# Attention in a two-layer trunk: the product of probabilities and V taken by key block for all 512 queries of a head

## The chip, the cores and the metric

The kernel runs on one core of a Trainium2 chip. The metric is the device time of one execution in microseconds. TensorE (PE) multiplies matrices into PSUM, VectorE (DVE), ScalarE (ACT) and GpSimd (POOL) do the work between the products, and SyncE (SP) issues the transfers.

## The reference

A trunk of two layers on 2048 frames of width 1024. Layer A is a gMLP mixer, which the change doesn't touch. Layer B is band attention with 16 heads of 64 channels: each chunk of 64 queries sees its own chunk and the eight before it, with a bias by clipped distance.

```python
def one_chunk(args):
    c, qc = args
    start = c * CHUNK
    kc = lax.dynamic_slice_in_dim(k_pad, start, B_BAND, axis=1)
    vc = lax.dynamic_slice_in_dim(v_pad, start, B_BAND, axis=1)
    sc = jnp.einsum('bqhd,bkhd->bhqk', qc, kc).astype(jnp.float32) + bias
    valid = (m + start) >= B_LEFT_PAD
    sc = jnp.where(valid[None, None, None, :], sc, NEG_INF)
    p = jax.nn.softmax(sc, axis=-1).astype(vc.dtype)
    return jnp.einsum('bhqk,bkhd->bqhd', p, vc)
...
return (o * jax.nn.silu(z)) @ w_out
```

All is float32, and the values need that accuracy.

## The kernel before

**Number format.** PE works on float32 values cut into a high and a low part (types F32R, made by a cast on ACT and a subtraction on DVE). A large product is three matmuls: high by high, low by high, high by low (`mm3`, lines 113 to 115, where most of PE's instructions therefore stand).

**Stages.** The mixer of layer A and the projection of V come first, up to some 1560 us. Then comes the attention, in four tiles of 512 queries (t), each with eight pairs of heads (p). For each pair there are eight steps u, four blocks of 128 queries for each of the two heads (`hd`, `qb`). A step issues, in this order of the source:

- `score`: the product of Q and K for the block two steps ahead (L1320), then on DVE the bias and the row maximum (L1328), on ACT the exponential with the row sum (L1335), on DVE its reciprocal (L1338), on POOL the scaling (L1339). A block of 128 queries sees 640 keys, in tile 0 fewer: 128 to 512, as there are no keys before.
- some products of the generators `ahead` (projections of Q, K and gate of the next pair, named pj) and `outs` (the output product of the tile before, named bo). They fill PE between the steps of the attention.
- `flip`: the probabilities of a block are transposed by PE in pieces of 128x128 into a scratch bank, of which there is one (`tp`, L1359); ACT casts them to the high part (L1362), DVE subtracts for the low part (L1363).
- at every second step `value`: the product with V (pv, lines 1380, 1381 and 1387).

**The product with V before.** It is taken for half a head, two blocks of queries (256 columns), with the half's own tile of transposed probabilities: [128, 2 parts, 6 key blocks, 256 queries]. There are two such tiles (tag PT, bufs=2). V stands as the stationary operand, 64 channels of the high part beside 64 of the low, so that the two halves of the result's partitions have to be added afterwards. The six key blocks of the half are not all seen by both query blocks: block 0 only by the first, block 5 only by the second. For tiles 1 to 3 these two are products of 2x128 columns which take the high and the low part side by side; the result is two sums (bank halves), the second of which holds only the low parts of the outer blocks:

```python
mm(po[:, :, 0:P], keys(0), pt[:, :, 0, 0:P], start=True, stop=False)
mm(po[:, :, P:256], keys(5), pt[:, :, 5, P:256], start=False, stop=False)
```

Then come four blocks of 256 columns for the high part and four for the low. ACT copies half of the partitions (L1399), DVE adds the other half (L1401) and then the two sums (L1406). In tile 0 all blocks are products of 256 columns; the part of block 5 that the first query block doesn't see is cleared by POOL (L1352), and L1401 alone makes the result.

**Order.** The program is written in the order above and a scheduler places the instructions of each engine by its own plan, so neighbours can change places. Every engine works off its queue in order; an instruction that waits holds up what is behind it. In tile 0 the weights of the projections come raw, are scaled on POOL (L184), cast on ACT (L199) and subtracted on DVE (L200), and the scaled ones are written back for the later tiles.

Of the kernel before, what the change touches and what calls it, by code (L numbers as in the profile page):

```python
# [17 lines left out]
P = 128  # L18
# [3 lines left out]
T = 512  # L22
# [11 lines left out]
def trunk_kernel(  # L34
# [19 lines left out]
    nc = tc.nc  # L54
# [42 lines left out]
    pmm = ctx.enter_context(tc.tile_pool(name="pmm", bufs=4, space=PSUM))  # L97
# [12 lines left out]
    mm, tpose = nc.tensor.matmul, nc.tensor.transpose  # L110
# [215 lines left out]
    with ExitStack() as actx:  # L326
# [492 lines left out]
        start = {}  # L819
# [8 lines left out]
        for n in range(6):  # L828
            for ph in PH:
# [4 lines left out]
                elif n > 2:  # L834
                    o = -13 if ph == 6 else -5
# [371 lines left out]
    with ExitStack() as bctx:  # L1207
        cb = bctx.enter_context(tc.tile_pool(name="cb", bufs=1, reuse_waits="tile"))
        sb = bctx.enter_context(tc.tile_pool(name="sb", bufs=2, reuse_waits="tile"))
# [6 lines left out]
        vtl = {}  # L1216
# [75 lines left out]
        pts = {}  # L1292
        og32s = {}
# [50 lines left out]
        def flip(t, p, u):  # L1344

            hd, qb = divmod(u, 4)
            h = 2 * p + hd
            g, qq = divmod(qb, 2)
            if qq == 0:
                pt = sb.tile([P, 2, 6, 256], F32R, tag="PT", name=f"pt{t}_{h}_{g}", bufs=2)  # L1350
                if t == 0:
                    nc.gpsimd.memset(pt[:, :, 5, 0:P].bitcast(F32), 0.0)  # L1352
                pts[t, h, g] = pt
            pt = pts[t, h, g]
            pr = prs[t, h, qb]
            b0 = 0 if t > 0 else 4 - qb
            tp = ptr.tile([P, KD, P], F32, tag="tr", name=f"tp{t}_{h}_{qb}")
            for b in range(b0, 5):
                tpose(tp[:, b, :], pr[:, b * P : (b + 1) * P], ident[:])  # L1359
            cs = slice(qq * P, (qq + 1) * P)  # L1360
            oh = pt[:, 0, b0 + qq : 5 + qq, cs]
            nc.scalar.copy(oh, tp[:, b0:5, :])  # L1362
            nc.vector.tensor_tensor(  # L1363
                pt[:, 1, b0 + qq : 5 + qq, cs], tp[:, b0:5, :], oh.bitcast(F32), op=ALU.subtract
            )

        def value(t, p, hd, g):

            h = 2 * p + hd
            pt = pts[t, h, g]  # L1370
            po = pmm.tile([P, 2, 256], F32, tag="mm", name=f"pv{t}_{h}_{g}")
            hs = slice(hd * P, hd * P + P)

            def keys(i):
                return vtl[t, p][:, 2 * g + i, hs]

            if t > 0:
                mm(po[:, :, 0:P], keys(0), pt[:, :, 0, 0:P], start=True, stop=False)  # L1380
                mm(po[:, :, P:256], keys(5), pt[:, :, 5, P:256], start=False, stop=False)
                blocks = range(1, 5)
            else:
                blocks = range(4 - 2 * g, 6)
            for j in range(2):
                for i in blocks:
                    mm(  # L1387
                        po[:, 0, :], keys(i), pt[:, j, i, :],
                        start=(t == 0 and j == 0 and i == blocks[0]),
                        stop=(j == 1 and i == blocks[-1]),  # L1390
                    )
            if hd == 0 and g == 0:
                og32s[t, p] = sb.tile([P, T], F32, tag="og32", name=f"og32_{t}_{p}", bufs=1)
            og32 = og32s[t, p]
            r, r2 = halves(hd)
            ot = sb.tile([P, 2, 256], F32, tag="ot", name=f"ot{t}_{h}_{g}", bufs=1)
            oq = og32[r, g * 256 : (g + 1) * 256]
            n = 2 if t > 0 else 1
            nc.scalar.copy(ot[r, :n, :], po[r2, :n, :])  # L1399
            o1 = ot[r, :, :] if t > 0 else oq  # L1400
            nc.vector.tensor_tensor(  # L1401
                o1, po[r, :n, :] if t > 0 else po[r, 0, :],
                ot[r, :n, :] if t > 0 else ot[r, 0, :], op=ALU.add,
            )
            if t > 0:
                nc.vector.tensor_tensor(oq, ot[r, 0, :], ot[r, 1, :], op=ALU.add)  # L1406
            if g == 0:
# [191 lines left out]
        def ahead(t, p):  # L1599

            if p + 1 < NPAIR:
                yield from project(t, p + 1)
                values(t, p + 1)
                if p == 0:
                    yield from gate(t, 0)
                yield from gate(t, p + 1)
                if t:
                    yield from some(outs[t - 1], SHARE[t][p])
            else:
                if t + 1 < NT:  # L1610
# [21 lines left out]
        before = None  # L1632
        for t in range(NT):
            for p in range(NPAIR):
                gen = ahead(t, p) if t + p else first
                total = steps_of(t, p) - (0 if t + p else 8)
                if t + 1 == NT and p + 1 == NPAIR:
                    last_open()
                per = 11 if p + 1 == NPAIR and t + 1 < NT else 16
                todo = []  # L1640
                if t == 0 and p in (2, 4):
                    todo = o_sums(p // 2 + 1, lambda n: half_tile("C", n, 4), lambda n: half_tile(
                        "S", n, 4, F32R
                    ))
# [24 lines left out]
                before = t, p  # L1669
        value(*before, 1, 1)  # L1670
        run(gen)
        while finals:
            finals.pop(0)()
# [58 lines left out]
```

## Time and profile before

| | |
|---|---|
| median of 3 runs | 2727.69 us (2720.04 to 2733.72) |
| profiled execution | 2731.61 us, span 2728.6 us |
| mean granted clock of TensorE | 0.986 |
| PE, DVE, ACT, POOL busy | 96%, 72%, 49%, 33% of the span |
| attention, tile 0 | from about 1560 to 1800 us |
| attention, tiles 1, 2, 3 | to about 2090, 2380, 2645 us |
| last output product | to the end |

The profile gives for each instruction its start and duration. Matmuls overlap in PE's pipeline, so that their durations add up to more than the time they take; the distance from one start to the next is what a matmul costs in a dense stretch. An idle time is shown with the instruction that ended it.

### The profile page before, as it was taken

How to read it: one execution, taken by the hardware profiler on the slowest of the kernel's cores; microseconds unless marked ns; L12 is line 12 of the kernel's file. 1: busy time of each engine (PE TensorE's matmuls, PEld its weight loads, DVE VectorE, ACT ScalarE, POOL GpSimd, SP SyncE). 2: the span in 40 equal slices, each digit the busy share in tenths (PEclk: the TensorE clock that was granted, in tenths of full speed). 3: DMA queues.
4: the chain of work that ended last, by engine and by line, in shares of the span. 5: the costliest groups of instructions: out<-in, count | busy, mean ns of one | idle time of the engine just before them, and what ended most of it. 6: DMA issues, size and time to landing. Idle time of an engine off the chain costs nothing. (4 is left out here: it accounts for less than half of the span.)

```text
span 2728.6 us, 38857 instructions
## 1 busy us (share of the span) xinstructions
PE 2630.1 (96%) x13216; PEld 2199.9 (81%) x13216; DVE 1961.0 (72%) x3097; ACT 1324.8 (49%) x2360; POOL 909.8 (33%) x906
## 2 busy tenths in 40 slices
PE   8999999999999999999989998999999999999997
PEld 7888888888888888888867776778887888788885
DVE  5655676676676669666677776677788778877787
ACT  5422242433424445332455465566656666666554
POOL 3512236142251414115143344322333223323243
PEclk9999999999999999999999999899999999999999
DMA  7899999989888879668667787766777667865567
GB/s 297 314 326 335 345 358 327 329 306 349 333 300 295 302 263 342 236 236 308 239 219 277 238 274 249 243 211 208 234 253 246 219 211 238 264 203 192 185 228 251
DMA packets 274773, 735.56 MB, mean 270 GB/s; under 512 B 29584, under 2 KB 61328, under 8 KB 274576
## 3 DMA queue, kind: packets, MB, share of 16 engines
q1 hardware_dynamic: 274576, 733.09, 77.9%
q8 instruction: 105, 1.72, 0.3%
q14 instruction: 92, 0.75, 0.1%
HBM read 540.56 MB, written 181.93 MB: 265 GB/s over the span
## 5 line engine op out<-in xcount | busy, mean ns | idle before, releaser
L113 PE MATMUL P<-T,S 128*128 128x512 f32 x1248 | 496.1, 398 | 2.7 <-ACT S L376 2.0
L115 PE MATMUL P<-T,S 128*128 128x512 f32 x1248 | 490.3, 393 | 0.0
L114 PE MATMUL P<-T,S 128*128 128x512 f32 x1248 | 489.1, 392 | 1.1 <-DVE T L379 1.1
L1339 POOL TENSOR_SCALAR pr<-pr,sl 128x640 f32<-128x640 f32 (+4 forms) x256 | 202.8, 792 | 553.9 <-DVE sl L1338 512.8
L113 PE MATMUL pj<-hh_b,wh_b 128*128 128x512 f32 x768 | 316.8, 412 | 7.7 <-ACT wh_b L199 6.7
L114 PE MATMUL pj<-hl_b,wh_b 128*128 128x512 f32 x768 | 307.4, 400 | 0.0
L115 PE MATMUL pj<-hh_b,wl_b 128*128 128x512 f32 x768 | 306.5, 399 | 0.0
L1335 ACT ACTIVATE pr<-pr,nm 128x640 f32<-128x640 f32 (+4 forms) x256 | 195.3, 763 | 222.4 <-DVE nm L1328 217.5
L115 PEld LDWEIGHTS P<-T,S 128*128 128x128 f32 x1248 | 235.4, 189 | 50.3
L113 PEld LDWEIGHTS P<-T,S 128*128 128x128 f32 x1248 | 235.9, 189 | 48.1 <-ACT S L376 2.3
L114 PEld LDWEIGHTS P<-T,S 128*128 128x128 f32 x1248 | 235.8, 189 | 46.9 <-DVE T L379 1.3
L1363 DVE TENSOR_TENSOR pt<-tp,pt 128x640 fp32r<-128x640 f32 (+4 forms) x256 | 188.8, 738 | 75.4 <-ACT pt L1362 73.1
L1328 DVE CUSTOM_DVE_ANT_0 pr<-s,bias 128x640 f32<-128x640 f32 (+4 forms) x256 | 188.2, 735 | 21.4 <-PE s L1320 15.6
L1362 ACT CAST pt<-tp 128x640 fp32r<-128x640 f32 (+4 forms) x256 | 158.6, 620 | 60.8 <-PE tp L1359 58.0
L1359 PEld LDWEIGHTS tp<-ident,pr 128*128 128x128 f32 x1120 | 135.1, 140 | 54.5 <-POOL pr L1339 15.9
L1359 PE MATMUL tp<-ident,pr 128*128 128x128 f32 x1120 | 165.8, 274 | 12.7 <-DVE pt L1363 6.5
L115 PEld LDWEIGHTS pj<-hh_b,wl_b 128*128 128x128 f32 x768 | 147.3, 192 | 32.6
L113 PEld LDWEIGHTS pj<-hh_b,wh_b 128*128 128x128 f32 x768 | 147.7, 192 | 27.5 <-ACT wh_b L199 8.3
L114 PEld LDWEIGHTS pj<-hl_b,wh_b 128*128 128x128 f32 x768 | 147.9, 193 | 17.3 <-issue 0.2
L1387 PE MATMUL pv<-pt,V 128*128 128x256 f32 x960 | 143.0, 289 | 11.2 <-ACT pt L1362 11.1
L200 DVE TENSOR_TENSOR wl_b<-raw_b,wh_b 128x1024 fp32r<-128x1024 f32 x96 | 122.9, 1280 | 42.4 <-ACT wh_b L199 41.2
L1387 PEld LDWEIGHTS pv<-pt,V 128*128 128x128 f32 x960 | 127.5, 193 | 14.9 <-ACT pt L1362 13.6
(291 smaller groups left out, 5941.5 us busy)
## 6 DMA issues: line engine op xcount, KB each, us to landing
S<-hsd SPq DMA_DIRECT2D x288, 512.0 KB, 5.5
rw<-in_w_a SPq DMA_DIRECT2D x108, 512.0 KB, 6.5
A<-ytd SPq DMA_DIRECT2D x72, 512.0 KB, 5.5
raw_b<-wk SPq DMA_DIRECT2D x72, 512.0 KB, 3.8
hsd<-S SPq DMA_DIRECT2D x56, 512.0 KB, 4.3
V<-vhd SPq DMA_DIRECT2D x56, 512.0 KB, 5.0
wh_bo<-ows SPq DMA_DIRECT2D x50, 512.0 KB, 4.5
wl_bo<-ows SPq DMA_DIRECT2D x50, 512.0 KB, 5.6
```

The costliest lines, as they stand in the source:

```text
L113: first = mm(ps, lh, rh, start=first, stop=False)
L114: mm(ps, lh, rl, start=False, stop=False)
L115: mm(ps, ll, rh, start=False, stop=last)
L200: tv(wl[:], raw[:], wh[:].bitcast(F32), op=sub)
L1328: nc.vector.tensor_tensor_reduce(out=pr[:, c0:].rearrange("p (a b) -> p a b", a=nseg), in0=ps[:, :nseg, :w], in1=bias[:, c0:].rearrange("p ...
L1335: nc.scalar.activation(pr[:, c0:], pr[:, c0:], AF.Exp, scale=-1.0, bias=nm[:], accum_out=sl[:])
L1339: nc.gpsimd.tensor_scalar(pr[:, c0:], pr[:, c0:], sl[:], 1.0, op0=ALU.mult, op1=ALU.mult)
L1359: tpose(tp[:, b, :], pr[:, b * P : (b + 1) * P], ident[:])
L1362: nc.scalar.copy(oh, tp[:, b0:5, :])
L1363: nc.vector.tensor_tensor(pt[:, 1, b0 + qq : 5 + qq, cs], tp[:, b0:5, :], oh.bitcast(F32), op=ALU.subtract)
L1387: mm(po[:, 0, :], keys(i), pt[:, j, i, :], start=(t == 0 and j == 0 and i == blocks[0]), stop=(j == 1 and i == blocks[-1]),)
```

## The change

One tile of transposed probabilities holds a whole head, [128, 5376]: the high parts of the four query blocks at 640 columns each, then the low parts (and room for a stride to run over). There is one such tile (bufs=1). `flip` writes each block to a contiguous stretch. `value` is called once for a head and goes by key block: block i of the eight (four in tile 0) is seen by query blocks q0 to q1, whose columns lie 512 apart in the tile, so that one product takes them all: 128, 256, 384 or 512 columns. High and low part of a block follow one another, and all is summed in one bank. The first block taken is one that all four query blocks see. Afterwards one copy on ACT and one addition on DVE, 64x512 each, make the head's result. The clearing on POOL falls away. The output rows (og32) get a second buffer.

In the loop, `value` of the first head stands ahead of `flip` at step 4, that of the second head ahead of `flip` at step 0 of the next pair; before, it stood behind `flip` at each even step.

```diff
-            g, qq = divmod(qb, 2)
-            if qq == 0:
-                pt = sb.tile([P, 2, 6, 256], F32R, tag="PT", name=f"pt{t}_{h}_{g}", bufs=2)
-                if t == 0:
-                    nc.gpsimd.memset(pt[:, :, 5, 0:P].bitcast(F32), 0.0)
-                pts[t, h, g] = pt
+            if qb == 0:
+                pts[t, h] = sb.tile([P, 5376], F32R, tag="PT", name=f"pt{t}_{h}", bufs=1)
...
-            oh = pt[:, 0, b0 + qq : 5 + qq, cs]
-            nc.scalar.copy(oh, tp[:, b0:5, :])
+            o = qb * 640
+            oh = pt[:, o + b0 * P : o + 640]
+            nc.scalar.copy(oh, tp[:, b0:5, :].rearrange("p a b -> p (a b)"))
...
-            if t > 0:
-                mm(po[:, :, 0:P], keys(0), pt[:, :, 0, 0:P], start=True, stop=False)
-                mm(po[:, :, P:256], keys(5), pt[:, :, 5, P:256], start=False, stop=False)
-                blocks = range(1, 5)
-            else:
-                blocks = range(4 - 2 * g, 6)
-            for j in range(2):
-                for i in blocks:
+            blocks = (3, 4, 0, 1, 2, 5, 6, 7) if t > 0 else (4, 5, 6, 7)
+            for i in blocks:
+                q0, q1 = max(0, i - 4), min(4, i + 1)
+                for j in range(2):
+                    o = j * 2560 + q0 * 512 + i * P
+                    rhs = pt[:, o : o + P]
+                    if q1 - q0 > 1:
+                        rhs = pt[:, o : o + (q1 - q0) * 512].rearrange("p (q c) -> p q c", c=512)
+                        rhs = rhs[:, :, 0:P]
                     mm(
-                        po[:, 0, :], keys(i), pt[:, j, i, :],
-                        start=(t == 0 and j == 0 and i == blocks[0]),
-                        stop=(j == 1 and i == blocks[-1]),
+                        po[:, q0 * P : q1 * P], vtl[t, p][:, i, hs], rhs,
+                        start=(i == blocks[0] and j == 0), stop=(i == 7 and j == 1),
                     )
...
-            nc.scalar.copy(ot[r, :n, :], po[r2, :n, :])
...
-            if t > 0:
-                nc.vector.tensor_tensor(oq, ot[r, 0, :], ot[r, 1, :], op=ALU.add)
+            nc.scalar.copy(ot[r, :], po[r2, :])
+            nc.vector.tensor_tensor(og32[r, :], po[r, :], ot[r, :], op=ALU.add)
...
+                    if u == 4:
+                        value(t, p, 0)
+                    elif u == 0 and before:
+                        value(*before, 1)
                     flip(t, p, u)
...
-                    if u % 2 == 0:
-                        if u:
-                            value(t, p, *divmod(u // 2 - 1, 2))
-                        elif before:
-                            value(*before, 1, 1)
```

More of the change, by code (lines that the diff above doesn't have):

```diff
@@ L1347, in flip @@
             h = 2 * p + hd
-            g, qq = divmod(qb, 2)
-            if qq == 0:
-                pt = sb.tile([P, 2, 6, 256], F32R, tag="PT", name=f"pt{t}_{h}_{g}", bufs=2)
-                if t == 0:
-                    nc.gpsimd.memset(pt[:, :, 5, 0:P].bitcast(F32), 0.0)
-                pts[t, h, g] = pt
-            pt = pts[t, h, g]
+            if qb == 0:
+                pts[t, h] = sb.tile([P, 5376], F32R, tag="PT", name=f"pt{t}_{h}", bufs=1)
+            pt = pts[t, h]
             pr = prs[t, h, qb]
@@ L1359, in flip @@
                 tpose(tp[:, b, :], pr[:, b * P : (b + 1) * P], ident[:])
-            cs = slice(qq * P, (qq + 1) * P)
-            oh = pt[:, 0, b0 + qq : 5 + qq, cs]
-            nc.scalar.copy(oh, tp[:, b0:5, :])
+            o = qb * 640
+            oh = pt[:, o + b0 * P : o + 640]
+            nc.scalar.copy(oh, tp[:, b0:5, :].rearrange("p a b -> p (a b)"))
             nc.vector.tensor_tensor(
-                pt[:, 1, b0 + qq : 5 + qq, cs], tp[:, b0:5, :], oh.bitcast(F32), op=ALU.subtract
+                pt[:, 2560 + o + b0 * P : 2560 + o + 640],
+                tp[:, b0:5, :].rearrange("p a b -> p (a b)"), oh.bitcast(F32), op=ALU.subtract,
@@ L1365, in flip, with value @@
             )
-        def value(t, p, hd, g):
+        def value(t, p, hd):
             h = 2 * p + hd
-            pt = pts[t, h, g]
-            po = pmm.tile([P, 2, 256], F32, tag="mm", name=f"pv{t}_{h}_{g}")
+            pt = pts[t, h]
+            po = pmm.tile([P, T], F32, tag="mm", name=f"pv{t}_{h}")
             hs = slice(hd * P, hd * P + P)
-            def keys(i):
-                return vtl[t, p][:, 2 * g + i, hs]
-            if t > 0:
-                mm(po[:, :, 0:P], keys(0), pt[:, :, 0, 0:P], start=True, stop=False)
-                mm(po[:, :, P:256], keys(5), pt[:, :, 5, P:256], start=False, stop=False)
-                blocks = range(1, 5)
-            else:
-                blocks = range(4 - 2 * g, 6)
-            for j in range(2):
-                for i in blocks:
-                    mm(
-                        po[:, 0, :], keys(i), pt[:, j, i, :],
-                        start=(t == 0 and j == 0 and i == blocks[0]),
-                        stop=(j == 1 and i == blocks[-1]),
-                    )
-            if hd == 0 and g == 0:
-                og32s[t, p] = sb.tile([P, T], F32, tag="og32", name=f"og32_{t}_{p}", bufs=1)
+            blocks = (3, 4, 0, 1, 2, 5, 6, 7) if t > 0 else (4, 5, 6, 7)
[7 more added lines that the diff above has]
+                        rhs = rhs[:, :, 0:P]
+                    mm(
+                        po[:, q0 * P : q1 * P], vtl[t, p][:, i, hs], rhs,
+                        start=(i == blocks[0] and j == 0), stop=(i == 7 and j == 1),
+                    )
+            if hd == 0:
+                og32s[t, p] = sb.tile([P, T], F32, tag="og32", name=f"og32_{t}_{p}", bufs=2)
@@ L1394, in value @@
             og32 = og32s[t, p]
             r, r2 = halves(hd)
[L1396 to L1404, printed above, removed]
@@ L1405, in value @@
-            if t > 0:
-                nc.vector.tensor_tensor(oq, ot[r, 0, :], ot[r, 1, :], op=ALU.add)
-            if g == 0:
+            ot = sb.tile([P, T], F32, tag="ot", name=f"ot{t}_{h}", bufs=1)
+            nc.scalar.copy(ot[r, :], po[r2, :])
+            nc.vector.tensor_tensor(og32[r, :], po[r, :], ot[r, :], op=ALU.add)
+            if hd == 0:
                 return
@@ L1669, in trunk_kernel @@
                 before = t, p
-        value(*before, 1, 1)
+        value(*before, 1)
         run(gen)
```

## The prediction

> **What bounds the kernel now.** I read the page's first two parts, then the table of stages, then the waits of TensorE in the first and in the later stages of the attention, and only then single products on the timeline. The page first: PE is busy nearly all of the span.
>
> ```profile
> PE 2630.1 (96%) x13216; PEld 2199.9 (81%) x13216; DVE 1961.0 (72%) x3097; ACT 1324.8 (49%) x2360; POOL 909.8 (33%) x906
> PEclk9999999999999999999999999899999999999999
> ```
>
> The change touches only the attention, which begins near 1560 us. The table of stages splits it: tile 0, tiles 1, 2, 3, and the tail. Columns after the stretch: its length, then busy time of PE, PEld, DVE, ACT, POOL, the granted clock and the DMA share.
>
> ```profile
> 1560.00:1800.00 240.00, 211.56 (x1054) 171.66 (x1052) 161.18 (x381) 138.33 (x311) 105.59 (x161) 0.94 0.77 248
> 1800.00:2090.00 290.00, 284.20 (x1615) 245.43 (x1615) 230.87 (x431) 178.94 (x320) 88.72 (x116) 0.99 0.72 233
> 2090.00:2380.00 290.00, 284.28 (x1624) 245.42 (x1623) 231.17 (x431) 180.90 (x323) 91.18 (x118) 0.99 0.72 232
> 2380.00:2645.00 265.00, 262.82 (x1516) 227.03 (x1515) 208.94 (x390) 161.31 (x294) 77.76 (x106) 1.00 0.62 198
> ```
>
> In tiles 1 to 3 PE is busy 98 to 99% at full clock and DVE, the next engine, some 80%: whatever PE has to do there is time. In tile 0 PE is idle 28 us and its clock is 0.94. The waits (microseconds in total, times, longest), first of 1560 to 1800, then of 1800 to the end:
>
> ```profile
> PE pv L1387 <- ACT pt L1362: 11.1, 5, 4.2
> PE tp L1359 <- DVE pt L1363: 3.5, 7, 0.9
> POOL pt L1352 <- PE pv L1387: 21.2, 13, 4.0
> ...
> PE s L1320 <- DVE nm L1328: 6.3, 5, 2.4
> PE tp L1359 <- DVE pt L1363: 3.0, 6, 0.9
> ```
>
> So tile 0 has waits at exactly the products that are changed; the later tiles have almost none on anything that is changed.
>
> **The products on PE.** A head of tiles 1 to 3 has 20 products of 256 columns (per half: two that take high and low part of an outer block side by side, then eight). After it has 16: four each of 512, 384, 256 and 128 columns. Both add up to 5120 columns. What counts is the step from one start to the next, because busy times of pipelined matmuls overlap. These rows of the timeline (start, duration) give the steps:
>
> ```profile
> 2003.17 1.12 PE L1387 MATMUL pv<-pt,V 128*128 128x256 f32 x8
> 2004.13 0.40 PE L113 MATMUL pj<-hh_b,wh_b 128*128 128x512 f32 x1
> ...
> 2005.52 0.45 PE L1320 MATMUL s<-K,Qh 128*128 128x320 f32 x2
> 2005.81 0.46 PE L1320 MATMUL s<-K,Ql 128*128 128x320 f32 x2
> 2006.10 0.39 PE L113 MATMUL pj<-hh_b,wh_b 128*128 128x512 f32 x1
> ...
> 1607.52 0.34 PE L1320 MATMUL s<-K,Qh 128*128 128x384 f32 x1
> 1607.70 0.35 PE L1320 MATMUL s<-K,Ql 128*128 128x384 f32 x1
> 1607.89 0.40 PE L113 MATMUL pj<-hh_b,wh_b 128*128 128x512 f32 x1
> ...
> 1747.53 0.39 PE L115 MATMUL pj<-hh_b,wl_b 128*128 128x512 f32 x1
> 1747.76 0.22 PE L1320 MATMUL s<-K,Qh 128*128 128x128 f32 x1
> 1747.82 0.28 PE L1320 MATMUL s<-K,Ql 128*128 128x128 f32 x1
> 1747.93 0.45 PE L113 MATMUL pj<-hh_b,wh_b 128*128 128x512 f32 x1
> 1748.21 0.39 PE L114 MATMUL pj<-hl_b,wh_b 128*128 128x512 f32 x1
> ```
>
> Columns of 256: (2004.13 - 2003.17) / 8 = 0.120 us. Of 512: the six products from 2004.13 to 2005.52 take 0.232 each. Of 320: (2006.10 - 2005.52) / 4 = 0.145. Of 384: 0.185 by the pair shown, 0.174 on the line between 320 and 512; I take 0.18. Of 128: a single step reads 0.06, but the next reads 0.11 and the product behind it starts late as well. From 1747.53 to 1748.21 there are two products of 512 and two of 128: 0.68 - 2 x 0.232 = 0.216, so 0.11 each. A product of 128 columns costs almost as much as one of 256, since the load of the next stationary tile does not fit under it; that is the cost that the change adds.
>
> The Trainium skill (TensorE: Matmul & The Clock Gate, Back-to-back issue gap) gives N / 2.4 + 2.5 ns between starts, 56 ns for 128 columns. By that estimate the sum below would be lower by some 12 us and the products a gain; the trace shows such a step only inside the pair and not for the pair as a whole, so the measurement decides.
>
> A head of tiles 1 to 3: before 20 x 0.120 = 2.40; after 4 x (0.232 + 0.18 + 0.12 + 0.11) = 2.57. That is +0.17 us for each of 48 heads, +8.1 us. A head of tile 0 has 12 products of 256 before (it multiplies a cleared block as well) and two of each width after: 1.44 against 1.28, -0.16 for each of 16 heads, -2.5 us. PE: **+5.6 us**. No row shows a 512-wide read in four pieces at a 2 KB pitch; two pieces of 128 (L1380) stand under the same 0.12 us, so I take no price. The 224 narrow products are the bound: at 0.06 each the sum falls by 11 to -6; at the price of 320 columns (0.145) it rises by 8 to +13.
>
> **What goes from DVE, ACT and POOL.** Groups of instructions (total, mean of one, idle before):
>
> ```profile
> L1401 DVE TENSOR_TENSOR ot<-pv,ot 64x512 f32<-64x512 f32 x96 | 65.7, 685 | 9.8 <-ACT ot L1399 8.2
> L1406 DVE TENSOR_TENSOR og<-ot 64x256 f32<-64x256 f32 x96 | 43.0, 448 | 2.7
> L1401 DVE TENSOR_TENSOR og<-pv,ot 64x256 f32<-64x256 f32 x32 | 13.4, 418 | 4.3 <-ACT ot L1399 3.8
> L1399 ACT COPY ot<-pv 64x512 f32<-64x512 f32 x96 | 55.9, 582 | 9.4 <-PE pv L1387 7.2
> L1399 ACT COPY ot<-pv 64x256 f32<-64x256 f32 x32 | 11.8, 368 | 3.7 <-PE pv L1387 2.9
> L1352 POOL MEMSET pt<- 128x256 f32 x32 | 10.1, 315 | 27.7 <-PE pv L1387 21.2 <-DVE Slv L286 3.2 <-issue 2.4
> ```
>
> DVE: 224 instructions, 122.1 us, become 64 additions of 64x512, 64 x 0.685 = 43.8: 78 us less. ACT: 67.7 us become 64 x 0.582 = 37.2: 30 us less. POOL loses 32 memsets of 10.1 us and the 21.2 us for which they stood at the head of its queue. Nearly all of it lies beside PE's work. What it can give is bounded by PE's waits on DVE in the later tiles, 6.3 + 3.0 us, most of which is not caused by the removed instructions; below nothing it cannot go, as no DVE instruction is added. I take **-2 us**. For POOL in tile 0: behind a waiting memset stand the normalisations (L1339) and the scaling of raw weights (L184), for which ACT and then PE wait. The 21.2 us are no price, since POOL was waiting for PE itself; I take **-2 us**, between nothing and the 11.1 us of PE's wait at the products.
>
> **The wait that moves.** The products stood behind the transposes of the next block; now they stand ahead of them, and with one probability tile (bufs=1) the copy of the next head's first block waits for the last product. That wait is free: on PE the products are already ahead of the transposes that the copy needs. Their second product needs the low half, so the subtraction on DVE, of the head's last block. In tiles 1 to 3 the transposes that stood at this place needed the same subtraction (the scratch bank of transposes is single), and they waited 3.0 us in all, so this costs nothing there. In tile 0 the four high products of 256 columns ran while DVE subtracted; now only one of 512 does, 0.48 - 0.23 = 0.25 us of cover less, on 16 heads at most 4 us; I take **+2 us**. Queued on ACT behind the copy that waits: exponentials and weight casts; they were behind the same transposes before.
>
> Also the spacing changes. Rows of PE and DVE in tile 1:
>
> ```profile
> 2016.50 0.71 PE L1359 MATMUL tp<-ident,pr 128*128 128x128 f32 x5
> 2016.96 0.48 PE L113 MATMUL bo<-wh_bo,Sho 128*128 128x512 f32 x1
> ...
> 2020.41 0.71 PE L1359 MATMUL tp<-ident,pr 128*128 128x128 f32 x5
> ...
> 2021.38 2.01 DVE L200 TENSOR_TENSOR wl_b<-raw_b,wh_b 128x1024 fp32r<-128x1024 f32 x1
> 2025.08 0.81 DVE L1363 TENSOR_TENSOR pt<-tp,pt 128x640 fp32r<-128x640 f32 x1
> 2026.04 0.74 PE L1359 MATMUL tp<-ident,pr 128*128 128x128 f32 x5 [0.38 <-DVE pt L1363]
> ```
>
> Between the transposes of neighbouring blocks lay some 3.4 us of other products (2016.96 to 2020.41), plus 1.2 us of products with V, ten at 0.120, at every second one. Now three come without and the fourth with 2.57. But the copy, the sum and the second addition (0.582, 0.685, 0.448) leave those windows too, so DVE's need falls with the cover. I price it at nothing; if DVE falls behind there, that is the second rival. SP's queue and the transfers keep their order in all that the sum uses; the second buffer of the output rows only removes a wait.
>
> **Sum.** +5.6 - 2 - 2 + 2 = +4 us. The profiled execution took 2731.61 us (span 2728.6 and 3.0 around it), so it would take 2735; it is 3.9 above the median 2727.69, to which the forecast belongs: **2732 us**. A measurement of this kernel can tell about 0.5%, 13.6 us, from no change, so the forecast is no change that can be told.
>
> **The rivals.**
> *Tile 0 recovers (faster).* With no memsets on POOL and fewer instructions on DVE, the 11.1 us at the products go, the transposes' 3.5 too, and half of what the clock lost (6% of 240 us, so 14, of which 7). That is -22, with the products' +5.6 it is -16 or so, in round numbers 2710. For it: 13 memsets waited for a product. Against: the longest waits of ACT in that tile are on raw weights (L184), which come by DMA and a POOL product of 1.9 us that remain.
>
> *DVE falls behind between value blocks (slower).* The rows above show the place: after the transposes at 2020.41, a weight split of 2.01 us comes ahead of the subtraction, which ends at 2025.89, and the next transposes wait although products with V lay between. Two blocks of each head lose 1.2 us of cover, 128 in all. It decides where the subtraction ends more than 3.4 us behind the transposes. If a quarter of them pay half of it, that is 32 x 0.6 = 19 us above the forecast: 2751. For it: such rows exist. Against: DVE has less to do, and only 13 such waits are in the whole stage now.
>
> *Fewer weight loads are a gain.* If each load of a stationary tile stood on the path, 256 products less at 0.11 us would give 28 us: 2700. The steps of 0.120 for 256 columns, load included, speak against it: a load is hidden there. The Trainium skill (TensorE: Matmul & The Clock Gate, The mechanism) says that loads overlap matmuls only in other row groups, which would put this rival first; the trace disagrees by those 0.120 us.
>
> **How the numbers follow.** Forecast 0.60 (of its own 2722 to 2742, from the narrow products' bounds, with 0.03 of it beyond the limit on the slow side); tile 0 recovers 0.12; weight loads 0.03; DVE behind 0.25. So faster 0.15, same 0.57, slower 0.28. The range leaves out about a tenth on either side: 2712 to 2752.
>
> **What would show it.** In the profile after: steps of 0.23, 0.18, 0.12 and 0.11 in the groups of products; PE's busy time in tiles 1 to 3 up by 2 to 3 us each with the same waits; DVE 78 and ACT 30 us less without a gain in the span. Wrong would be: steps of 0.06 behind the narrow products; a tile 0 that is more than 10 us shorter; or waits of transposes and products on the subtraction (L1363's successor) of over 15 us.

## The result and the profile after

| | before | after |
|---|---|---|
| median of 6 runs each | 2726.3 us (2720.0 to 2733.7) | 2711.9 us (2709.7 to 2715.6) |
| profiled execution, span | 2731.6, 2728.6 us | 2711.3, 2709.6 us |

The ratio is 0.9955, with a 95% interval of 0.9941 to 0.9968: 12 us faster by the ratio and 14 by the medians, where 2732 us was forecast. That is just below the forecast's range, and faster by more than the measurement is uncertain, though by a little less than 0.5%.

The first part of the page of the changed kernel has the DVE, ACT and POOL work gone as expected (DVE 79 us less, ACT 29, POOL 20):

```profile
PE 2624.9 (97%) x12960; PEld 2194.7 (81%) x12960; DVE 1882.2 (69%) x2937; ACT 1295.4 (48%) x2296; POOL 890.3 (33%) x874
```

The stages are cut here at the first transposes of each tile, since the tiles lie elsewhere after. Length, then busy time of PE, PEld, DVE, ACT, POOL, granted clock, DMA share, GB/s. First the kernel before, then after, tiles 0 to 3:

```profile
1569.00:1804.00 235.00, 209.01 (x1050) 170.21 (x1049) 161.28 (x381) 135.40 (x308) 102.78 (x158) 0.94 0.76 247
1804.00:2099.00 295.00, 289.22 (x1645) 249.42 (x1644) 235.24 (x441) 183.71 (x328) 90.65 (x119) 0.99 0.72 234
2099.00:2393.00 294.00, 287.85 (x1642) 248.12 (x1641) 234.87 (x439) 182.87 (x326) 91.21 (x119) 0.99 0.72 231
2393.00:2667.00 274.00, 267.87 (x1552) 231.43 (x1551) 217.55 (x408) 166.02 (x306) 89.68 (x117) 1.00 0.64 207
```

```profile
1566.00:1788.00 222.00, 205.19 (x995) 165.81 (x995) 159.81 (x365) 134.07 (x293) 94.12 (x127) 0.95 0.80 263
1788.00:2080.00 292.00, 288.68 (x1583) 249.53 (x1582) 214.16 (x395) 175.54 (x316) 90.45 (x120) 0.99 0.71 235
2080.00:2373.00 293.00, 288.44 (x1580) 248.15 (x1579) 213.38 (x390) 173.41 (x311) 90.23 (x119) 0.99 0.72 232
2373.00:2648.00 275.00, 266.64 (x1470) 228.09 (x1468) 193.99 (x359) 156.65 (x288) 87.21 (x117) 1.00 0.64 207
```

Tile 0 is 13 us shorter, 9 of it PE's idle time (26.0 to 16.8 us) and 4 its busy time; tiles 1 to 3 are some 3 us shorter in all, and PE's busy time there has not risen by the 2 to 3 us a tile that were forecast. The profiled execution of before is a long one in tile 0: two other kernels with the same order of instructions on every engine but POOL (b_big and b_ms2 in the table below) had 229.0 and 228.1 us there, the changed kernel and one of its order (a_memset) 220.8 and 219.5, so about 7 to 9 of the 13 belong to the change.

**PE's steps.** One head of tile 1 in the changed kernel (start, duration):

```profile
2021.50 0.39 PE L115 MATMUL pj<-hh_b,wl_b 128*128 128x512 f32 x1
2021.73 2.66 PE L1379 MATMUL pv<-pt,V 128*128 128x512 f32 x16
2024.22 0.73 PE L1355 MATMUL tp<-ident,pr 128*128 128x128 f32 x5
```

The sixteen products take 2024.22 - 2021.73 = 2.49 us, forecast 2.57, before 2.40. The single starts of this head give 0.227 for 512 columns and 0.176 for 384. A product of 128 columns is followed after 0.057 or 0.067, but what stands behind is late: the second product of 128 takes 0.113 or 0.110, and the one of 256 behind such a pair 0.170, where 256 columns else take 0.118 to 0.127. The eight products of 256 and 128 columns take 0.88 us together, forecast 4 x (0.12 + 0.11) = 0.92.

**The waits of PE.** In tile 0 the wait of the products (11.1 us before) has shrunk; in tiles 1 to 3 (1788 to 2648) that of the transposes on the subtraction has grown from 3.0 to 9.0, while the waits of scores on DVE's row maximum (6.3 before) and of projections on weight casts (4.8 before) have shrunk (microseconds, times, longest):

```profile
PE pv L1379 <- ACT pt L1358: 3.0, 4, 2.1
...
PE tp L1355 <- DVE pt L1359: 9.0, 6, 2.8
PE s L1320 <- DVE nm L1328: 1.9, 2, 1.7
PE pj L113 <- ACT wh_b L199: 0.7, 1, 0.7
```

**One stall in tile 0.** Here is the longest wait of the kernel before on ACT, with POOL and PE beside it. The last number in brackets is the idle time before and what ended it:

```profile
1662.22 0.60 ACT L1250 ACTIVATE Qh<-pj 64x512 fp32r<-64x512 f32 x1
1667.86 1.04 ACT L199 CAST wh_b<-raw_b 128x1024 fp32r<-128x1024 f32 x1 [5.04 <-POOL raw_b L184]
1668.92 0.59 ACT L1250 ACTIVATE Qh<-pj 64x512 fp32r<-64x512 f32 x1
1669.54 0.51 ACT L1335 ACTIVATE pr<-pr,nm 128x256 f32<-128x256 f32 x1
...
1670.17 0.59 ACT L1362 CAST pt<-tp 128x512 fp32r<-128x512 f32 x1
...
1664.68 1.29 POOL L315 TENSOR_TENSOR wo<-wo,wo 128x512 f32<-128x512 f32 x1
1665.93 1.90 POOL L184 TENSOR_TENSOR raw_b<-raw_b,bg 128x1024 f32<-128x1024 f32 x1
...
1666.18 0.39 PE L115 MATMUL pj<-hh_b,wl_b 128*128 128x512 f32 x1
1670.81 0.74 PE L1387 MATMUL pv<-pt,V 128*128 128x256 f32 x4 [4.24 <-ACT pt L1362]
```

The transposes of head 6's last block were done, but their copy (1670.17) stood in ACT's queue behind a cast of the gate's weights for pair 4 (1667.86), which waited 5.0 us for POOL; POOL was busy with sums of output weights (L310 to L315). PE waited 4.24 us for the copy, and the granted clock was then 0.50 for 3.4 us:

```profile
1671.50:1674.90 3.40, 3.35 (x12) 2.60 (x11) 1.64 (x6) 1.24 (x4) 1.72 (x4) 0.50 0.81 266
```

In the changed kernel the copy stands ahead of the same cast. ACT still waits there, but PE waits for nothing that stands behind it:

```profile
1659.25 0.51 ACT L1335 ACTIVATE pr<-pr,nm 128x256 f32<-128x256 f32 x1
...
1659.87 0.59 ACT L1358 CAST pt<-tp 128x512 fp32r<-128x512 f32 x1
...
1662.03 1.05 ACT L199 CAST wh_b<-raw_b 128x1024 fp32r<-128x1024 f32 x1 [1.56 <-POOL raw_b L184]
...
1661.58 1.38 PE L1379 MATMUL pv<-pt,V 128*128 128x512 f32 x8
1662.80 0.29 PE L1355 MATMUL tp<-ident,pr 128*128 128x128 f32 x1
```

The diff doesn't touch this cast. The scheduler planned another order; what in the change led it there isn't shown.

### The profile page after: what moved, and what is told of

Same layout as the page of the kernel before. It is cut to its first block, busy times and chain, and to the rows that moved or that the text cites. A ratio compares the mean times of both kernels' runs of the same rounds, so it can differ in the third digit from the quotient of the medians.

```text
span 2709.6 us, 38048 instructions
## 1 busy us (share of the span) xinstructions
PE 2624.9 (97%) x12960; PEld 2194.7 (81%) x12960; DVE 1882.2 (69%) x2937; ACT 1295.4 (48%) x2296; POOL 890.3 (33%) x874
## 5 line engine op out<-in xcount | busy, mean ns | idle before, releaser
L1379 PEld LDWEIGHTS pv<-pt,V 128*128 128x128 f32 x896 | 145.2, 191 | 24.6 <-ACT pt L1358 6.1
L1379 PE MATMUL pv<-pt,V 128*128 128x256 f32 (+3 forms) x896 | 156.1, 323 | 5.6 <-ACT pt L1358 3.7
```

What stands on the lines that cost most here:

```text
L1379: mm(po[:, q0 * P : q1 * P], vtl[t, p][:, i, hs], rhs, start=(i == blocks[0] and j == 0), stop=(i == 7 and j == 1),)
```

## The experiments

Each was timed beside the kernel before on the same chip; the tile lengths are from its profiled execution, between the first copies of transposed probabilities of the tiles ("rest": tile 3 and the end). Lengths of one order vary by up to some 2 us a tile between executions, tile 0 by up to 5.5.

| kernel | ratio to before, 95% | tile 0 | 1 | 2 | rest |
|---|---|---|---|---|---|
| before | 1 | 233.6 | 294.7 | 294.0 | 334.9 |
| after | 0.9955 (0.9941 to 0.9968) | 220.8 | 291.7 | 292.9 | 335.7 |
| a_memset | 0.9964 (0.9948 to 0.9979) | 219.5 | 292.0 | 293.4 | 338.5 |
| b_nomemset | 0.9969 (0.9959 to 0.998) | 220.0 | 295.5 | 294.2 | 335.0 |
| b_ahead | 0.999 (0.9978 to 1.0001) | 228.1 | 293.0 | 292.5 | 340.2 |
| a_t0 | 0.996 (0.9947 to 0.9972) | 218.9 | 293.4 | 294.9 | 335.9 |
| b_big | 0.9992 (0.998 to 1.0005) | 229.0 | 295.2 | 294.7 | 336.0 |
| b_clear1 | 0.9989 (0.9977 to 1.0001) | 226.4 | 293.7 | 293.5 | 333.9 |
| b_ms2 | 0.9999 (0.9986 to 1.0011) | 228.1 | 295.4 | 294.3 | 335.3 |
| b_place | 0.9991 (0.9981 to 1.0) | 227.2 | 292.8 | 293.6 | 336.6 |
| b_cast | 0.9977 (0.9967 to 0.9988) | 223.7 | 295.8 | 294.5 | 334.5 |
| a_dve | 1.0003 (0.9993 to 1.0014) | 217.5 | 295.7 | 298.0 | 343.5 |
| a_spread | 1.0018 (1.0008 to 1.0029) | 217.4 | 298.3 | 296.9 | 343.7 |
| a_dveonly | 1.0016 (1.0007 to 1.0025) | 219.5 | 295.4 | 295.5 | 342.2 |
| a_actonly | 0.9981 (0.997 to 0.9991) | 219.8 | 294.2 | 294.0 | 340.1 |
| b_noadd | 0.9961 (0.9947 to 0.9975) | 232.5 | 287.7 | 289.1 | 335.1 |
| b_clump | 1.0036 (1.0024 to 1.0048) | 227.6 | 301.1 | 297.0 | 333.0 |
| a_hifirst | 0.9955 (0.9941 to 0.9969) | 216.9 | 290.8 | 292.4 | 338.7 |
| a_castall | 1.0057 (1.0044 to 1.007) | 245.3 | 293.4 | 291.2 | 338.0 |
| a_ogpool | 0.9974 (0.9962 to 0.9985) | 224.8 | 292.2 | 295.1 | 336.5 |

### Which part: tile 0 alone

a_t0: `(flip if t else flip0)(t, p, u)`, and the same for `value`: the changed scheme in tile 0 only.

> Tile 0 in the changed kernel's way, tiles 1 to 3 in the way of before, in one persistent probability tile of 6144 columns that both share; output rows in one buffer. If the gain lies in tile 0, as the two profiles show (13 of 19 us), this run is 10 to 14 us faster than before, 2712 to 2716. If tiles 1 to 3 carry it (fewer instructions on DVE and ACT), 4 us or less faster than before. The persistent tile may move the scheduler's order by some us either way.

Measured 0.996: nearly the whole gain is that of tile 0.

### Is it the clearing on POOL?

a_memset puts two clearings for each head of tile 0 into the changed kernel, on the unused end of the tile (first lines); b_nomemset takes them from the kernel before, with the products that needed them narrowed (the other lines):

```diff
+            if t == 0 and qb % 2 == 0:
+                nc.gpsimd.memset(pt[:, 5120:5376].bitcast(F32), 0.0)
...
-                    nc.gpsimd.memset(pt[:, :, 5, 0:P].bitcast(F32), 0.0)
+                    c = slice(P if t == 0 and i == 5 else 0, 256)
-                        po[:, 0, :], keys(i), pt[:, j, i, :],
+                        po[:, 0, c], keys(i), pt[:, j, i, c],
```

> The changed kernel with the clearing on POOL put back: in tile 0, two memsets of 128x256 a head, into the unused end of the probability tile, at the head's first and third block. Nothing else changes its place on any engine. Theory M (the memsets at the head of POOL's queue held up the scaling of weights and probabilities in tile 0): most of tile 0's gain of 13 us is lost, the run is 8 to 13 us slower than the changed kernel, 2720 to 2725. Theory P (the gain comes from where and how the products stand): within 3 us of the changed kernel, 2709 to 2715.

> The kernel before without the clearing on POOL in tile 0: the outer key block of a half is taken with the 128 columns that see it, so that nothing has to be cleared. Theory M: 8 to 13 us faster than before, 2713 to 2718. Theory P: within 3 us of before.

Clearing put back costs at most a few microseconds. Leaving it out and halving the width of the products on block 5 gave 8 us, but the scheduler's order changed with it, so this run doesn't tell which. Three kernels kept the order of PE, ACT and DVE, but for one pair of neighbours on PE in b_clear1: b_big (one persistent tile, the control), b_clear1 (its zero part cleared once instead of 32 times), b_ms2 (each clearing twice).

> Control for the persistent tile: the kernel before with its two probability tiles as two halves of one tile, memsets and all else as before and in the same order on each engine. Within 3 us of before by both theories; more would be a price or a gain of the way in which tiles are released.

> The kernel before with its two probability tiles in one persistent tile, and the part that has to be zero in tile 0 cleared once at the start (nothing writes there later). The 32 memsets are gone from POOL's queue and nothing else changes its place on any engine; the products are those of before. Theory M (memsets that wait at the head of POOL's queue for a product): 7 to 10 us faster than before, 2716 to 2720. Theory P (the products): within 3 us of before.

> The kernel before with each memset of tile 0 issued twice: 10 us more work on POOL, the same waits for products, all else in its place. If POOL's work is what costs (32 x 0.315 us), some 3 to 8 us slower than before. If the wait ahead of the first memset is what costs, the second one is nearly free: within 3 us of before.

With the order fixed, clearing two times, one time or not at all for each half lie within 3 us, and the 20 us for which POOL waited with its clearing (22.3 in b_big, none in b_clear1) were worth nothing that can be told. This theory fell.

### Is it the place of the products?

b_ahead takes the products ahead of the transposes at every even step; b_place takes both halves of a head together at the place of the changed kernel, in tile 0 only, with the zero part cleared once:

```diff
+                    if t == 0 and u == 4:
+                        value(t, p, 0, 0)
+                        value(t, p, 0, 1)
```

> The kernel before with the products with V ahead of the transposes of the next block at each even step, as the changed kernel has them; products, tiles, clearing and additions as before. Theory M: no gain, within 3 us of before. Theory P in the form that the place counts: 8 us or more faster than before.

> The kernel before, with the zero part of the probability tile cleared once (no clearing on POOL in the heads) and in tile 0 both halves' products of a head taken together ahead of the transposes of the next head, where the changed kernel has them; still 256 columns for each product, two sums, copies and additions by halves. ACT's order keeps the weight cast of the gate of pair 4 ahead of the copy of head 6, block 3. Theory 'the planner's order': the wait of that cast stays, tile 0 takes 226 to 229 us, the ratio is 0.998 to 1.000. Rival 'place of the products': tile 0 takes 219 to 222 us as in the changed kernel, the ratio is about 0.996.

Tile 0 stayed at 227 to 228 us. The place is not it, and ACT's cast stood ahead of the copy in both.

### The order on ACT's queue

b_cast is the kernel before with one order added between the cast of the stall and the copy:

```diff
+        if (t, p, c) == (0, 4, 2):
+            tc.add_manual_dep(hi.ins, copies[0, 6, 3], ...)
```

> The kernel before with one instruction moved: on ACT's queue in tile 0, the cast of the gate's weights of pair 4 (L199) is ordered behind the copy of the transposed probabilities of head 6, block 3; in the kernel before the planner put it ahead of that copy, where it waited 5.0 us for POOL's scaling, with the copy, and so a product with V that waited 4.2 us, queued behind it. In the changed kernel the cast stands behind the copy. POOL's order is the same, PE's differs by a few neighbours. Theory 'the planner's order': this one cast is most of the gain in tile 0. The stall of some 4.3 us in the fourth pair goes and with it half of a window of 3.4 us at half clock: tile 0 is 5 to 6 us shorter than in the kernel before (about 223 us), the fourth pair 31 to 26 us, the ratio 0.998. Rival 'place of the products': tile 0 stays at 228 to 230 us, the ratio at 0.999 to 1.000. Rival 'another wait takes its place': the wait on ACT goes but the fourth pair stays above 29 us.

Measured 0.9977, 6 us (3 to 9); the fourth pair takes 27.3 us instead of 31.5. (Some neighbours on PE and DVE changed places with it.) Its ACT queue:

```profile
1661.40 0.59 ACT L1258 ACTIVATE Qh<-pj 64x512 fp32r<-64x512 f32 x1 [1.16 <-DVE Ql L1259]
...
1662.64 0.59 ACT L1370 CAST pt<-tp 128x512 fp32r<-128x512 f32 x1
1665.28 1.05 ACT L201 CAST wh_b<-raw_b 128x1024 fp32r<-128x1024 f32 x1 [2.05 <-POOL raw_b L186]
```

Four places on one queue are worth half of the whole gain. The traces of the other kernels agree. Where the cast stands ahead of the copy and waits 3.8 to 5.2 us for POOL (before, b_big, b_clear1, b_ms2, b_clump, b_noadd, b_ahead, b_place), the fourth pair of tile 0 takes 29.9 to 32.1 us, from its first copy to that of the next pair. In the changed kernel and its seven relatives that have the cast behind the copy and no further order added, it takes 24.4 to 25.1. In b_nomemset the cast is ahead, but waits only 1.1 us; PE's stall there is 1.99 us instead of 4.24, and the pair takes 29.1.

a_castall asks whether the rule is general: every weight cast of tile 0 goes behind the copy that the program has before it.

```diff
+        if t == 0 and last_copy:
+            tc.add_manual_dep(hi.ins, last_copy[-1], ...)
```

> The changed kernel with every weight cast of tile 0 on ACT (L199) ordered behind the copy of transposed probabilities that stands last before it in the program, so that no cast that waits for POOL's scaling holds up such a copy. Theory 'one cast made the stall': the changed kernel has that cast behind already, so little is left; products with V waited 3.0 us in tile 0; between 3 us faster and 6 us slower than the changed kernel, as projections now wait for later casts; the ratio is 0.9945 to 0.998. Rival 'every cast ahead of a copy costs': 5 us or more faster than the changed kernel, the ratio below 0.9935.

It is not: 28 us slower than the changed kernel, outside both expectations, since PE now waits for the weights: "PE pj <- DVE wl_b" is 13.8 us in its tile 0.

### What DVE's and ACT's work is worth in tiles 1 to 3

a_dve puts the amount of work that fell away back in one clump behind the products; a_spread puts it at the places where the kernel before had it:

```diff
+            if u % 4 == 2:
+                nc.scalar.copy(ot[r2, :], ot[r, :])
+                nc.vector.tensor_tensor(ot[r, :], ot[r, :], ot[r, :], op=ALU.add)
+            nc.vector.tensor_tensor(ot[r, 0:256], ot[r, 0:256], ot[r, 256:T], op=ALU.add)
```

> The changed kernel with the work on ACT and DVE after the products put back for tiles 1 to 3: for each head one more copy of 64x512 on ACT, one more addition of 64x512 and two of 64x256 on DVE (76 us of DVE, 28 us of ACT in all), with no use of their results. If the relief of DVE is what made tiles 1 and 2 shorter (by 4 us, although their products cost 2.4 us more each), those tiles are 5 us or more longer in sum and the run 5 to 10 us slower than the changed kernel, 2717 to 2722. If not, within 3 us of the changed kernel.

> The changed kernel with DVE and ACT work of the kernel before put back in tiles 1 to 3 as dummy work on finished data, at the places where the kernel before had it: behind the transposes of the third block of each head one copy 64x512 on ACT and additions 64x512 and 64x256 on DVE, behind those of the first block one addition 64x256. An earlier run with the same amount in one clump behind the products lost 15 us. Theory 'less work on DVE and ACT pays for the narrow products': the amount counts, not the clump; tiles 1 to 3 take 8 to 13 us more than in the changed kernel, the ratio is about 1.000. Rival 'clump': spread over the head the work hides, as DVE is busy 69 per cent only; tiles 1 to 3 take 0 to 4 us more, the ratio is 0.9955 to 0.997. My forecast's own term, 2 us, goes with the rival.

Both lose the whole gain, more than was expected of either; a_spread lies 17 us above the changed kernel (1.0018 - 0.9955 = 0.0063, of 2725) with DVE's work at 1970 us (before: 1961). The waits of its PE in tiles 1 to 3 show where:

```profile
PE tp L1355 <- DVE pt L1359: 17.3, 16, 3.8
PE s L1320 <- DVE nm L1328: 4.0, 4, 2.8
```

Then DVE's and ACT's part alone, and the opposite in the kernel before (b_noadd: `n = 1` and no second addition):

> The changed kernel with only the DVE part of the work put back in tiles 1 to 3, at the places of the kernel before (per head one addition 64x512 and two of 64x256, no copy on ACT). Both parts together cost 18 us. Theory 'it is DVE, whose subtraction and row maximum PE waits for': 10 us or more over the changed kernel, the ratio 0.9995 to 1.002. Rival 'it is ACT': less than 5 us, the ratio 0.9955 to 0.9975.

> The changed kernel with only the ACT part of the work put back in tiles 1 to 3 (per head one copy 64x512, at the place of the kernel before). Theory 'it is DVE': 0 to 4 us over the changed kernel, the ratio 0.9955 to 0.997. Rival 'it is ACT': 10 us or more, the ratio 0.999 to 1.001.

> The kernel before with DVE and ACT work left out behind the products of tiles 1 to 3: of the two sums of a half head only the first is taken (copy and addition 64x256 instead of 64x512, the second addition L1406 not at all). What is left out is the low part of the outer key blocks. PE's products are unchanged. DVE has some 85 us less to do, ACT some 28, about as much as the change takes away. Theory 'the work on DVE counts': tiles 1 to 3 take 6 to 15 us less than in the kernel before, the ratio is 0.995 to 0.998. Forecast (2 us): the ratio is 0.999 to 1.000.

DVE's part alone costs 17 us, ACT's alone 7, between the two expectations, both together 17: the parts overlap. In the kernel before, leaving such work out gives 11 us. The forecast's 2 us were far too small either way.

b_noadd's gain lies in two places, the last pair of tiles 1 and 2: 34.2 and 34.8 us instead of 40.3 and 40.1. Here is that place in tile 1 of the kernel before, two waits of PE and the stretch behind them:

```profile
2065.54 0.56 PE L1320 MATMUL s<-K,Qh 128*128 128x320 f32 x2 [2.39 <-DVE nm L1328]
2068.41 0.80 PE L113 MATMUL pj<-hh_b,wh_b 128*128 128x512 f32 x1 [2.01 <-ACT wh_b L199]
2067.50:2074.20 6.70, 5.79 (x14) 4.59 (x15) 5.92 (x13) 2.29 (x4) 4.94 (x6) 0.50 0.96 297
```

The granted clock was 0.50 for 6.7 us. In b_noadd PE waits in this stretch once, for 1.86 us, and the clock stays at 1.00 (2059 to 2073). So the work that was left out had cost more here than PE's wait on DVE: a wait on a weight cast besides, and half of the clock behind both.

### What the place costs in tiles 1 to 3

b_clump is b_place for tiles 1 to 3 (tile 0, products and additions as before):

> The kernel before with one persistent probability tile, and in tiles 1 to 3 both halves' products of a head taken together ahead of the transposes of the next head, where the changed kernel has them. All 20 products of 256 columns, the copies and the additions are as before; tile 0 is as before. Theory 'lost cover' (the second rival of the prediction: with ten products less between two blocks' transposes, DVE's subtraction is late): waits of transposes on the subtraction rise from 3 us to above 10 us, tiles 1 to 3 take 8 to 14 us more than in the kernel before, the ratio is 1.003 to 1.005. Rival 'the dummy work has a price of its own': tiles 1 to 3 take 0 to 3 us more, the ratio is 0.999 to 1.001.

It is 10 us slower (7 to 13; 12 against its control b_big), in tiles 1 and 2. The wait that grew is the one that the second rival names (3.0 us before):

```profile
PE tp L1361 <- DVE PT L1365: 12.3, 8, 3.5
```

But it isn't spread over the heads, as lost cover alone would be. The second to sixth pairs of tiles 1 and 2 take no longer than before (182.2 and 182.8 us, before 183.2 and 183.3). Of the 12.3 us, 8.6 are waits of the second block of a head, 0.8 of the fourth, which lost as much cover. The longest two, 3.02 and 3.47 us, are in the last pair of tiles 1 and 2; the first of them:

```profile
2060.23 1.42 DVE L1541 SCALAR_TENSOR_TENSOR y<-y,rr_f,gf 128x512 f32<-128x512 f32 x2 [2.75 <-DMA y<-x2d]
...
2061.75 0.42 DVE L1408 TENSOR_TENSOR og<-ot 64x256 f32<-64x256 f32 x1
2062.21 0.82 DVE L1365 TENSOR_TENSOR PT<-tp,PT 128x640 fp32r<-128x640 f32 x1
...
2063.18 0.74 PE L1361 MATMUL tp<-ident,pr 128*128 128x128 f32 x5 [3.02 <-DVE PT L1365]
```

DVE's subtraction (L1365) stands behind the scaling of finished output rows (y), which waited 2.75 us for a transfer, and behind a sum of the products (og). In the kernel before the subtraction at this place came ahead of y, and the sums behind it:

```profile
2060.13 0.82 DVE L1363 TENSOR_TENSOR pt<-tp,pt 128x640 fp32r<-128x640 f32 x1
2062.04 1.78 DVE L1539 SCALAR_TENSOR_TENSOR y<-y,rr_f,gf 128x512 f32<-128x512 f32 x2 [1.10 <-issue]
```

The two longest waits of the changed kernel, 2.83 and 2.84 of its 9.0 us, are at the same two places with y and the sum ahead in the same way. The 10 us are thus the price of the place; a good part of it is the order on DVE's queue, and what the lost cover alone costs isn't shown.

### Two other versions

a_hifirst (`for j in range(2)` outside `for i in blocks`) and a_ogpool (`nc.gpsimd.tensor_tensor(og[:], og32[:], zt[t, p][:], op=ALU.mult)`):

> The changed kernel with the products of a head in another order: all high parts first, then all low parts, so that eight products (some 1.2 us) instead of one (0.23 us) lie ahead of the first that needs DVE's subtraction. Theory of the forecast (the cover of that subtraction was cut by 0.25 us on the heads of tile 0, at most 4 us): 0 to 4 us faster than the changed kernel, the ratio to the kernel before 0.994 to 0.9955. Rival (the products' second instruction does not wait): the same as the changed kernel within 2 us. As the stationary tile then changes with each product, a loss of more than 3 us would show that high and low behind the same stationary tile gain something.

> The changed kernel with the product of the output rows and the gate (L1396, 30 instructions of 0.88 us, 26 us) moved from DVE to POOL; its factor 0.5 goes into the copy on ACT and the addition on DVE, which stay one instruction each. Theory 'each us of DVE work in tiles 1 to 3 costs about 0.2 us': 4 to 6 us faster than the changed kernel, the ratio to the kernel before 0.993 to 0.9945. Rival 'POOL's queue': an instruction of some 1.3 us on POOL, which waits for DVE's addition, stands ahead of the scalings of probabilities for which the transposes wait, 30 times; the ratio is 0.9955 to 0.998, and waits of transposes on POOL's scaling appear in tiles 1 to 3.

The order of high and low parts makes no difference. Taking 26 us more from DVE by giving them to POOL is 5 us slower than the changed kernel: the rival's loss, but not at its place. The transposes' wait on POOL's scaling in the later tiles is unchanged (2.6 us, 2.4 in the changed kernel). The profiled execution loses 4 us in tile 0, where POOL's busy time rises from 94 to 103 us. Its fourth pair takes 27.9 us instead of 24.4: the weight cast stands ahead of the copy again and waits 0.92 us for POOL, and PE waits 1.54 us for the copy. No version was found that beats the changed kernel.

## Why the prediction was wrong, step by step

- **PE's products, +5.6 us: direction right, size too large.** By the steps measured it is (2.49 - 2.40) x 48 = +4.3 in tiles 1 to 3; in tile 0 the eight products take 1.22 us (1661.58 to 1662.80 above), so 1.22 - 1.44 = -0.22 on 16 heads, -3.5: +1 in all. The price of 0.11 for 128 columns was about right, if what stands late behind them is counted; the excess of 0.08 us a head comes from all widths by a little. Of the signs named for an error, steps of 0.06 did appear, but the next product made up for each. The Trainium skill (TensorE: Matmul & The Clock Gate, Back-to-back issue gap) has, beside the formula weighed in the prediction, which it gives for an isolated matmul, measured spacings for streams of loads and matmuls: about 81 ns for 128 columns, with which the mean step of 87 in the head above nearly agrees, and 131 ns for 512, with which the 227 here don't.
- **Relief of DVE and ACT, -2 us: a term that failed.** It was bounded by PE's waits on DVE in the trace of before, 9 us, and most of these were judged unrelated. The work removed is worth 11 us in the kernel before and 17 in the changed one. The bound left out what b_noadd shows in the last pair of tiles 1 and 2: a wait on a weight cast that goes too, and the half clock behind the waits.
- **Spacing of the products, priced at nothing: wrong too, the other way.** b_clump prices it at +10 us. The prediction took it that the sums on DVE leave the windows that lose cover. In the window behind a head's first block they came in, ahead of the subtraction, and 8.6 of the 12.3 us of waits are there. The second rival named the right wait, but as a loss in many heads; it came in a few places, in good part from the order on DVE's queue, and in the changed kernel the work removed more than makes up for it.
- **Clearing on POOL, -2 us:** 0 to 6 by b_clear1's interval; nothing that can be told.
- **The wait that moves, +2 us:** a_hifirst, which gives the cover back, is not faster: nothing.
- **Tile 0: the sum priced every queue in its old order.** In the profile it came 13 us shorter, and more than 10 had been named as a sign of being wrong. The first rival gave 2710 us, and the time was that, but by luck: it came not from the clearing, but from the place of one cast on ACT, 6 us by b_cast, and the clock that was to recover in tile 0 stayed where it was (0.94, then 0.95). The argument set against this rival, that ACT's longest waits are on raw weights and remain, named the right wait and drew the wrong conclusion: it remained, and what stood behind it changed.

The miss divides by a_t0, which changes tile 0 alone. There the forecast was -2.5 - 2 + 2 = -2.5 us and the run shows -11 (0.996). That leaves -1 for tiles 1 to 3, where +8.1 - 2 = +6 was forecast: the two large terms that were wrong there, relief and spacing, mostly cancel each other.

The pieces in one sum: cast -6, place +10, DVE and ACT work -11 to -17, products +1, clearing -3 to 0 gives -6 to -15, measured -12 (by the ratio). Each is from its own kernel and they need not add. That the cast is a cause in the changed kernel is shown from the other side, by b_cast; a kernel that differs from the changed one only by the cast ahead of the copy is not among the runs, though in a_ogpool, which has it ahead, the fourth pair loses 3.5 us. b_cast takes 4.2 us off the fourth pair and the change 7.1; where the other 3 come from stays open. And b_nomemset's tile 0 of 220.0 us, with the cast ahead, shows that the scheduler has other orders as good: its cast waits less, but why POOL is ready sooner and why the pairs around it are shorter stays open too.

## What to carry to other kernels

Compare the order of instructions on every queue before and after, also for those that the diff doesn't touch: a wait that stays can become harmless or costly by what stands behind it. An engine that is 80% busy and feeds the one at 99% is not free: price its work by leaving some out, not by the waits that a trace shows now. Price such work at the places where the waits gather, with the half clock that may follow them, and not evenly over all heads: here the last pair of two tiles held all that was gained by leaving work out, and more than half of what was lost by moving products.

## What was not expected of the hardware

A product of 128 columns started 0.057 to 0.067 us before the next, and the product behind the pair paid for it (0.170 us instead of 0.118 for 256 columns). A common block of V is not the reason: in a_hifirst, where neighbours within a pass have different blocks, the step behind a product of 128 columns is 0.06 us as well, and a head takes the same 2.49 us.

After PE had stood idle for 4.24 us, the granted clock was 0.50 for 3.4 us from soon after its restart, so by an estimate (half of 3.4) the stall cost some 1.7 us on top of itself. The Trainium skill (TensorE: Matmul & The Clock Gate, Part 1: The HAM clock gate) says that the clock falls to half after an idle window of about 3.4 us and needs as long a stretch of work to return. The trace agrees with the second in this place. The first is not the least idle time that suffices here: in the changed kernel PE waited 1.99 us (until 1645.87), and the granted clock was 0.50 from 1646.3 to 1649.6.
